# Three edits to one core's conformer block: where the first up-projection sums stand on VectorE, where a third pair of up products runs, and where one down-projection weight is split

## The chip, the cores and the metric

The kernel runs on one core of one Trainium2 chip. The metric is the device time of one execution in microseconds; it is given as a median over runs. Every time of a single instruction comes from one execution that the hardware profiler recorded. The engines are called as the profile calls them: PE (TensorE matmul), PEld (TensorE weight load), DVE (VectorE), ACT (ScalarE), POOL (GpSimd), SP (SyncE, which here only starts DMA transfers; its queue is shown as SPq).

## The reference

One conformer block on x of 1 x 1024 tokens x 1024 channels, float32 throughout, one layer:

```python
h = rms_norm(x, norm1_g)
glu_in, q, k, v, gate_logits = split(h @ w_in)
a = a_val * sigmoid(a_gate)
a = silu(rms_norm(causal_depthwise_conv(a, conv_w, conv_b), conv_norm_g))   # 31 taps
y_a = a @ w_conv_out
y_b = o @ w_attn_out          # o: 16 heads, three dilation groups mixed by softmax of their lse
g_a, g_b = split(sigmoid(gate_logits + gate_b))
x = x + (g_a * y_a + g_b * y_b) @ w_out
h = rms_norm(x, norm2_g)
u = causal_depthwise_conv(h @ w_up, ffn_conv_w, ffn_conv_b)                 # 3 taps, 5632 columns
u_val, u_gate = split(u)
x = x + (silu(u_gate) * u_val) @ w_down                                     # 2816 rows
```

The edits lie in the last third: the merge of the two branches and `w_out`, the up projection, and the start of the down projection.

## The kernel before, in words

**Products of float32.** Each operand is split into a high part and a low part (`split`, L74 to L77: ACT copies the high part to the fp32r type at L76, DVE subtracts it from the source at L77), and each product is three matmuls: high by high, high by low, low by high. Weights come from memory in pieces of 128 x 1024 (`stage`, L81), and pass through three tags of four buffers each: `raw`, `whi`, `wlo`. PSUM has two tiles of two banks (`big_ps`) and four single banks (`bank_ps`).

**Engines and order.** All DMA transfers are started by SP, one queue in program order. Every engine works through its own program in order. Most of that order is made by a planner when the kernel is built, from the written order, the costs it assumes and the free buffers; so an instruction may stand ahead of one that was written before it. Two things bind it: inside `tc.manual_schedule` (L797 to L891) ACT, DVE and PE keep the written order, and `tc.issue_after(ins)` puts what is written under it behind `ins`. Where a buffer is used again, the new writer waits for the last reader.

**Merge and w_out.** `merge(c, w, half)` (L607 to L625) loads two gates and y_a for eight channel blocks and two halves of the tokens (L611 to L613), takes two sigmoids (L614, L615), multiplies y_a by its gate (L616), computes y_b with PE, multiplies it by the other gate (L623), adds (L624) and splits the sum into `mT`, the left operand of `w_out`. `wo_piece(j, i)` (L627 to L637) stages a quarter of half of `w_out` and splits it (L632 ACT, L633 DVE). The merges of the last two blocks are followed by the token loop `for tt in range(8)` (L718 to L722): 24 matmuls (L125 to L127) for each of eight token tiles and the first 512 columns, added to x (L704), written to `dx2`. A second round, over the second 512 columns, ends with the norm and scaling (`wo_scaled`, L715) and the transposes (`transpose_raw`, L686, copied out at L687).

**Forms ahead.** The up projection takes each pair of column tiles (f and 22 + f, 256 columns in all) by seven products of a 512 x 128 weight block with a 512 x 512 activation block in place of eight, which needs sums of weight blocks. For f = 0 and 1 these sums are made ahead, during `w_out`: `forms_ahead(f)` (L653 to L678) loads two pieces, forms sums on DVE (L661), splits them and spills the parts to memory (`dform`), from which `fetched` brings them back later. For f = 1 the plain piece is split and spilled too.

**Up projection.** A tile has two plain products (`up_first`, L752: 12 matmuls each into two banks, X and Z) and five with sums (`y` and `xz` at L740 to L742). The right operands are sums of the activations, held in blocks t1, t2, t3, t4, b22 (high part on ACT at L791, low part on DVE at L794, the sums at L822). The hand-ordered stretch makes these blocks for the first half of the tokens, transposes the last two token tiles (x6, x7), runs the plain products of f = 1 (`xz1`), makes the second half of the blocks, and then runs the five products of f = 0 (`y_0`, then the X products; `xc`, L877, copies a product out of its bank before the next one adds to it). From then on tiles run one behind another: `up_rest` (L910 to L931; its last copy out of a bank is L930), with `up_weights`, `up_first` and `up_sums` (L760 to L771) for the tile after it.

**Start of the down projection.** Before the last up tile two pairs of `early` tiles load and split the first two groups of activations. Then, for each group of two feature tiles, `wload` (L933 to L941) loads a piece of `w_down`, `wsplit` splits it through `whi` and `wlo` (`hi_a`, `lo_a`), and `mac` (L993, tiles `dx` and `dy`) multiplies; the third group's activations are split into `gh` and `gl`.

## Time and profile before

| | |
|---|---|
| median of 3 runs | 1802.28 us (1801.72 to 1803.02) |
| profiled execution | 1801.54 us |
| its span | 1799.8 us |
| mean granted TensorE clock | 0.996 |
| PE | 1764.8 us busy, 98%, 8248 instructions |
| DVE | 1314.3 us busy, 73%, 1805 |
| ACT | 770.4 us busy, 43%, 1203 |
| POOL | 182.9 us busy, 10%, 193 |
| DMA | 270.16 MB, mean 150 GB/s |

The span runs from the first to the last instruction that the profiler recorded; the execution's time has 1.7 us around it. A row of the timeline reads: start and length in us, engine, line and operation, result <- operands by the program's names, shapes, how many such instructions stand together, and in brackets how long the engine had been idle before it and what released it. A row of the windows view gives a stretch, its length, then the busy time (and count) of PE, PEld, DVE, ACT and POOL, the granted clock of PE (1.00 is full), the share of time that the DMA engines worked, and GB/s. A matmul's own length overlaps with the next one's; the distance between starts is what it costs.

### The profile page before, as it was taken

The numbers are of one execution on the slowest core, as the hardware profiler recorded it, in microseconds if no ns is written. First come the engines' busy times: TensorE is split into PE (matmuls) and PEld (weight loads), VectorE is DVE, ScalarE is ACT, GpSimd is POOL, SyncE is SP. The second block draws the span as 40 slices with busy tenths as digits, with TensorE's granted clock in tenths as the row PEclk, the third lists the DMA queues.
The fourth block names the chain that finished last, engine by engine and source line by source line (L and its number), as shares of the span: only waits on it lengthen the run. The fifth ranks groups of instructions, "written<-read, shape, count | busy, mean of one in ns | idle before, by whom it ended". The sixth has DMA issues, their size and how long they took to land.

```text
span 1799.8 us, 22541 instructions
## 1 busy us (share of the span) xinstructions
PE 1764.8 (98%) x8248; PEld 1460.0 (81%) x8248; DVE 1314.3 (73%) x1805; ACT 770.4 (43%) x1203; POOL 182.9 (10%) x193
## 2 busy tenths in 40 slices
PE   8999999999999999999999989999999999999999
PEld 6888888888887888878888878778888888878887
DVE  6999999999635666665654554687777677679863
ACT  5111132232246666665654333455454454543431
POOL 1000132133003222122210000000000000000000
PEclk9999999999999999999999999999999999999999
DMA  5111145345468546674527556532222222389851
GB/s 205 50 52 51 39 137 171 104 138 161 146 207 250 141 137 182 197 210 135 153 71 268 180 205 242 193 105 91 85 71 94 83 78 86 118 322 330 289 181 47
DMA packets 145809, 270.16 MB, mean 150 GB/s; under 512 B 11681, under 2 KB 60961, under 8 KB 145698
## 3 DMA queue, kind: packets, MB, share of 16 engines
q1 hardware_dynamic: 145696, 268.72, 46.1%
q8 instruction: 65, 1.06, 0.2%
q14 instruction: 46, 0.38, 0.1%
q10 hardware_dynamic: 2, 0.00, 0.0%
HBM read 196.32 MB, written 72.35 MB: 149 GB/s over the span
## 4 chain that ended last, share of the span: by engine, by line
PE 55%; DVE 4%; DMA 3%; ACT 1%; issue 1%; SPq 0%; POOLq 0%; DVEq 0%; ACTq 0%
PE dx L993 6%; PE xz L741 5%; PE xz L740 5%; PE xz L742 5%; PE dy L993 5%; DMA gg<-dya 2%; PE pp L524 2%; PE y L741 2%; PE y L740 2%; PE y L742 2%; PE ya L108 2%; PE ya L109 2%; PE ya L110 2%; PE o L532 2%; PE o L533 1%; PE wo L126 1%
## 5 line engine op out<-in xcount | busy, mean ns | idle before, releaser
L367 DVE SCALAR_TENSOR_TENSOR cacc<-apad,pk,cacc 128x1024 f32<-128x1024 f32 x240 | 297.9, 1276 | 0.7
L125 PE MATMUL qkv<-hi_qkv,hT 128*128 128x512 f32 x384 | 151.9, 397 | 0.0
L127 PE MATMUL qkv<-hi_qkv,hT 128*128 128x512 f32 x384 | 150.5, 392 | 0.0
L126 PE MATMUL qkv<-lo_qkv,hT 128*128 128x512 f32 x384 | 149.5, 390 | 0.0
L513 DVE CUSTOM_DVE_ANT_0 p<-s,m 128x128 f32<-128x128 f32 (+7 forms) x128 | 95.1, 750 | 62.5 <-PE pp L524 42.7
L77 DVE TENSOR_TENSOR pl<-pp,ph 128x512 fp32r<-128x512 f32 x192 | 102.9, 550 | 47.6 <-ACT ph L76 47.0
L76 ACT ACTIVATE ph<-pp 128x512 fp32r<-128x512 f32 x192 | 91.2, 488 | 94.7 <-PE pp L524 92.0
L517 POOL TENSOR_SCALAR p<-p,st 128x128 f32<-128x128 f32 (+7 forms) x128 | 95.2, 753 | 332.5 <-DVE st L516 269.8
L903 DVE SCALAR_TENSOR_TENSOR u<-u,pk 128x1023 f32<-128x1023 f32 x88 | 112.2, 1276 | 2.7 <-ACT u L901 2.5
L101 POOL TENSOR_TENSOR rs<-ss,mhalf 128x8 f32<-128x8 f32 x32 | 73.8, 2312 | 337.9 <-DVE ss L100 337.9
L515 ACT ACTIVATE p<-p,st 128x128 f32<-128x128 f32 (+7 forms) x128 | 99.0, 776 | 14.9 <-DVE st L513 13.1
L108 PE MATMUL gate<-hT,hi_gt 128*128 128x512 f32 x256 | 101.5, 396 | 0.0
L109 PE MATMUL gate<-hT,hi_gt 128*128 128x512 f32 x256 | 100.5, 393 | 0.0
L110 PE MATMUL gate<-hT,lo_gt 128*128 128x512 f32 x256 | 100.0, 392 | 0.0
L524 PE MATMUL pp<-ident,p 128*128 128x128 f32 x576 | 93.8, 276 | 0.0
L127 PEld LDWEIGHTS qkv<-hi_qkv,hT 128*128 128x128 f32 x384 | 72.1, 188 | 15.4
L126 PEld LDWEIGHTS qkv<-lo_qkv,hT 128*128 128x128 f32 x384 | 72.2, 188 | 14.4
L125 PEld LDWEIGHTS qkv<-hi_qkv,hT 128*128 128x128 f32 x384 | 72.2, 188 | 14.0
L77 DVE TENSOR_TENSOR lo_uv<-raw_uv,hi_uv 128x1024 fp32r<-128x1024 f32 x21 | 25.7, 1226 | 78.2 <-ACT hi_uv L76 78.2
L524 PEld LDWEIGHTS pp<-ident,p 128*128 128x128 f32 x576 | 69.1, 141 | 10.0 <-issue 0.2
L532 PE MATMUL o<-ph,v 128*128 128x512 f32 x192 | 73.0, 380 | 3.9 <-ACT ph L76 1.7
L508 PE MATMUL s<-kh,q 128*128 128x512 f32 (+1 forms) x192 | 68.4, 361 | 7.3 <-DVE st L513 7.2
(307 smaller groups left out, 4632.8 us busy)
## 6 DMA issues: line engine op xcount, KB each, us to landing
wr<-w_down SPq DMA_DIRECT2D x45, 512.0 KB, 5.5
gr<-dff SPq DMA_DIRECT2D x62, 256.0 KB, 5.1
raw_qkv<-w_qkv SPq DMA_DIRECT2D x24, 512.0 KB, 3.9
dff<-u SPq DMA_DIRECT2D x22, 512.0 KB, 2.6
raw_uv<-w_up SPq DMA_DIRECT2D x21, 512.0 KB, 3.2
raw_ug<-w_up SPq DMA_DIRECT2D x20, 512.0 KB, 3.2
dv<-v SPq DMA_DIRECT2D x16, 512.0 KB, 3.2
raw_gt<-w_ch SPq DMA_DIRECT2D x16, 512.0 KB, 4.6
```

What stands on the lines that cost most here:

```text
L77: dve.tensor_tensor(out=lo, in0=src, in1=hi.bitcast(F32), op=ALU.subtract)
L108: pe.matmul(o, hi[:, k, :], ah[:, k, :], start=(k == 0), stop=False)
L109: pe.matmul(o, hi[:, k, :], al[:, k, :], start=False, stop=False)
L110: pe.matmul(o, lo[:, k, :], ah[:, k, :], start=False, stop=(k == KT - 1))
L125: pe.matmul(ps, ah, hi[:, k % 2, :], start=(k == 0), stop=False)
L126: pe.matmul(ps, ah, lo[:, k % 2, :], start=False, stop=False)
L127: pe.matmul(ps, al, hi[:, k % 2, :], start=False, stop=(k == KT - 1))
L367: dve.scalar_tensor_tensor(out=acc, in0=a[:, j : j + T], scalar=w(j), in1=acc, op0=ALU.mult, op1=ALU.add)
L524: pe.transpose(pp[:, qb * P : (qb + 1) * P], pts[qb][:, kt * P : (kt + 1) * P], ident)
L740: pe.matmul(o, wh[:, k, :], bh[:, k, :], start=(start and k == 0), stop=False, skip_group_check=not start)
L741: pe.matmul(o, wh[:, k, :], bl[:, k, :], start=False, stop=False, skip_group_check=not start)
L993: pe.matmul(banks[n], a[:, c], b[:, d], start=(start and i == 0 and m == 0), stop=(stop and i == nf - 1 and m == 2), skip_group_check=True)
```

## The change

Three edits.

1. `merge` returns the two instructions of its split. `forms_ahead` is called after token tiles 0, 2 and 3 (for f = 0, 1, 2) and everything it issues on an engine is queued behind the two split instructions of the last merge (block 7, second half).
2. `forms_ahead(2)` only loads the plain piece of f = 2, splits it and spills its two parts. The hand-ordered stretch fetches them (`w2`) and runs that pair's 24 matmuls into two single banks (`xz2`) between `xz1` and `y_0`. The transposes of x6 and x7 are written between the halves of `xz1`, ahead of the high part of t2; the low part of t2's first half is written later, behind the second half's first low part. For f = 2 the loop then only makes the sums, without its own `up_weights` and `up_first`.
3. The two `early` tiles get a fourth row. Before the last up tile the second group's first weight piece is loaded and split into those rows; its place among the `whi` and `wlo` buffers at the start of the down projection goes.

By engine, the program has as many PE and DVE instructions as before, and five more DMA transfers on SP: one load, two spills and two fetches.

```diff
@@ gate and memory tiles
-    dform = [[dr.tile([P, 1024], F32R, name=f"dform{f}_{i}") for i in range(7)] for f in range(2)]
+    dform = [[dr.tile([P, 1024], F32R, name=f"dform{f}_{i}") for i in range(7)] for f in range(3)]
@@ merge
-                split(mT[0][half][:, c, :], mT[1][half][:, c, :], ya)
+                hi, lo = mT[0][half][:, c, :], mT[1][half][:, c, :]
+                return (act.activation(hi, ya, AF.Copy),
+                        dve.tensor_tensor(out=lo, in0=ya, in1=hi.bitcast(F32), op=ALU.subtract))
...
-            merge(7, ws[3], 1, lambda b: wo_first.append(wo_piece(0, 3, b)))
+            merged = merge(7, ws[3], 1, lambda b: wo_first.append(wo_piece(0, 3, b)))
@@ forms_ahead
-            v, g = stage(w_up[f], f"fv{f}"), stage(w_up[FT + f], f"fg{f}")
-            t = hb2.tile([P, 4, 1024], F32R, tag=f"hb{f}1", name=f"form{f}")
-            r = hb2.tile([P, 4, 1024], F32R, tag="hb10", name=f"formr{f}")
+            v = stage(w_up[f], f"fv{f}")
+            r = hb2.tile([P, 4, 1024], F32R, tag="hb00" if f == 2 else "hb10", name=f"formr{f}")
+            if f < 2:
+                g = stage(w_up[FT + f], f"fg{f}")
+                t = hb2.tile([P, 4, 1024], F32R, tag=f"hb{f}1", name=f"form{f}")
+            else:
+                g = v
...
             if f:
                 split(r[:, 2], r[:, 3], v)
+            if f == 2:
+                for i in range(2):
+                    spill(dform[f][5 + i], r[:, 2 + i])
+                return
...
-            if tt in (0, 2):
-                forms_ahead(tt // 2)
+            if tt in (0, 2, 3):
+                with tc.issue_after(merged[0].ins), tc.issue_after(merged[1].ins):
+                    forms_ahead((tt + 1) // 2)
@@ up projection
+        def up_half(o, w, i):
+            product(o, four(w[0])[:, 4 * i : 4 * i + 4], four(w[1])[:, 4 * i : 4 * i + 4], *left[i], True)
...
             w1 = fetched(1, 5, "uv")
+            w2 = fetched(2, 5, "uv")
...
+            transpose_raw(x6, 6)
+            xz1 = big_ps("xz_1")
+            up_half(xz1[:, 0:512], w1, 0)
+            transpose_raw(x7, 7)
+            up_half(xz1[:, 512:1024], w1, 1)
             high("t2", t3[0], q)
             act.activation(xc[:, 0:512], xz0[:, 0:512], AF.Copy)
-            transpose_raw(x6, 6)
-            transpose_raw(x7, 7)
-            low("t2", t3[0], q)
...
-            xz1 = up_first(1, w1)
+            xz2 = [bank_ps(f"xz_2{i}") for i in range(2)]
+            for i in range(2):
+                up_half(xz2[i], w2, i)
...
             low("t1", t1[1], q)
+            low("t2", t3[0], cols[0])
             high("b22", b22[:, :, cols[0]], cols[0])
...
-            X, Z = xz[:, 0:512], xz[:, 512:1024]
+            X, Z = xz if f == 2 else (xz[:, 0:512], xz[:, 512:1024])
@@ loop over the up tiles
-        early = []
+        early, rooms = [], []
...
-                    e = hb2.tile([P, 3, 1024], F32R, tag=f"hb{a}1", name=f"early{a}")
+                    e = hb2.tile([P, 4, 1024], F32R, tag=f"hb{a}1", name=f"early{a}")
+                    rooms.append(e[:, 3])
...
+                split(*rooms, wload(0, 0, groups[1], wp))
...
-                if 1 < f + 1 < FT:
+                if f == 1:
+                    ready.append((xz2,) + up_sums(2, stage(w_up[2], "uv2")))
+                elif 2 < f + 1 < FT:
                     v, w = up_weights(f + 1)
                     ready.append((up_first(f + 1, w),) + up_sums(f + 1, v))
@@ down projection, first loop
-            w = wload(0, 0, fs, wp)
-            if fs is groups[1]:
+            if fs is not groups[1]:
+                w = wload(0, 0, fs, wp)
+            else:
                 rs11 = [residual(0, n, 0) for n in range(4)]
             g = early.pop(0) if early else gsplit(gload(0, 0, fs), f"b11_{fs[0]}")
-            first2.append((g, wsplit(w, f"a11_{fs[0]}")))
+            first2.append((g, rooms if fs is groups[1] else wsplit(w, f"a11_{fs[0]}")))
```

More of the change, by code (lines that the diff above doesn't have):

```diff
@@ L750, in up_weights @@
             return v, wsplit(v, f"uv{f}")
+        def up_half(o, w, i):
+            product(o, four(w[0])[:, 4 * i : 4 * i + 4], four(w[1])[:, 4 * i : 4 * i + 4], *left[i], True)
         def up_first(f, w):
-            vh, vl = w
             xz = big_ps(f"xz_{f}")
-            product(xz[:, 0:512], four(vh)[:, 0:4], four(vl)[:, 0:4], *left[0], True)
-            product(xz[:, 512:1024], four(vh)[:, 4:8], four(vl)[:, 4:8], *left[1], True)
+            for i in range(2):
+                up_half(xz[:, i * 512 : i * 512 + 512], w, i)
             return xz
@@ L851, in block_kernel @@
             blk = {n: (t[:, 0], t[:, 1]) for n, t in blocks.items()}
-            xz1 = up_first(1, w1)
+            xz2 = [bank_ps(f"xz_2{i}") for i in range(2)]
+            for i in range(2):
+                up_half(xz2[i], w2, i)
             q = cols[1]
```

## The prediction

> **What bounds the kernel now.** I read the page's first lines, then the table of what TensorE (PE) waited for over the whole run, then PE's, DVE's and ACT's timelines around each wait that the diff can touch.

> ```profile
> PE 1764.8 (98%) x8248; PEld 1460.0 (81%) x8248; DVE 1314.3 (73%) x1805; ACT 770.4 (43%) x1203; POOL 182.9 (10%) x193
> ```

> PE is busy 98% of the span, and by the built program the change leaves its instructions as many as they were. So time can come only from places where PE stands or its clock is low. In the waits (total us, times, longest) three places belong to the edited lines:

> ```profile
> PE wo L126 <- DVE lo_wo L633: 4.6, 1, 4.6
> PE tq L686 <- issue: 1.7, 1, 1.7
> PE dx L993 <- ACT u L930: 1.4, 1, 1.4
> PE y L741 <- DVE blk_t L794: 0.8, 1, 0.8
> PE xz L741 <- DVE blk_t L794: 0.8, 1, 0.8
> PE xz L740 <- ACT blk_t L791: 0.7, 1, 0.7
> PE xz L740 <- ACT xc L877: 0.7, 1, 0.7
> PE dx L993 <- DVE gl_b L77: 0.4, 1, 0.4
> PE dx L993 <- ACT gh_b L76: 0.3, 1, 0.3
> ```

> They are A, the start of w_out (4.6); C, the hand-ordered start of the up projection (`tq`, `y`, `xz`, 4.7 named); D, the start of the last projection (`dx`, 2.1). Every profile time below is on the clock of the profiled execution, 1801.54 us, 0.74 under the runs' median of 1802.28.

> **A. Form sums tied behind merge 7.** DVE runs in its programmed order; so does PE.

> ```profile
> 1055.08 0.68 DVE L623 TENSOR_TENSOR gg<-yb,gg 128x512 f32<-128x512 f32 x1
> 1060.20 0.69 DVE L661 TENSOR_TENSOR formr<-raw_fg 128x512 f32<-128x512 f32 x1 [4.44 <-DMA raw_fg<-w_up]
> 1060.81 0.68 DVE L624 TENSOR_TENSOR gg<-gg 128x512 f32<-128x512 f32 x1
> 1061.41 1.22 DVE L633 TENSOR_TENSOR lo_wo<-raw_wo,hi_wo 128x1024 fp32r<-128x1024 f32 x1
> ...
> 1057.67 0.39 PE L125 MATMUL wo<-hi_wo,mT 128*128 128x512 f32 x1
> 1062.68 0.79 PE L126 MATMUL wo<-lo_wo,mT 128*128 128x512 f32 x1 [4.62 <-DVE lo_wo L633]
> ...
> 1068.67 0.39 PE L127 MATMUL wo<-hi_wo,mT 128*128 128x512 f32 x1
> ...
> 1757.89 5.44 PE dy L993 x24
> ```

> A form sum (L661) waited 4.44 for its w_up piece and held up the merge and lo_wo_2, for which PE then stood 4.62. Afterwards PE ran at half pace. From the row of 24 in the chain of waits, an undisturbed matmul costs 5.44 / 24 = 0.2267. The one at 1068.67 is the 15th after the one at 1057.67, so undisturbed it begins at 1057.67 + 15 x 0.2267 = 1061.07: 7.60 are lost here, 4.6 standing and 3.0 slow. The windows view shows the slow part as granted clock (0.57, behind POOL's pair):

> ```profile
> 1062.60:1069.40 6.80, 6.72 (x18) 5.29 (x19) 6.80 (x10) 3.25 (x4) 0.00 (x0) 0.57 0.72 211
> ```

> With L661 behind both splits of merge 7, L624 follows L623 at 1055.7 and lo_wo_2 is done at 1057.55; PE wants it at 1057.90. What is late next is piece 3, behind merge 7 on ACT:

> ```profile
> 1054.95 0.39 PE L125 MATMUL wo<-hi_wo,mT 128*128 128x512 f32 x1
> ...
> 1052.97 0.42 SPq L613 DMA_DIRECT2D gg<-dya  x1
> ...
> gg<-dya SPq DMA_DIRECT2D x1, 256.0 KB, 5.9
> ...
> 1058.28 0.63 ACT L615 ACTIVATE gg<-gg 128x512 f32<-128x512 f32 x1 [1.51 <-DMA gg<-dgate]
> 1062.06 1.04 ACT L632 ACTIVATE hi_wo<-raw_wo 128x1024 fp32r<-128x1024 f32 x1
> ```

> Merge 7's own transfers do not move: its second sigmoid still starts at 1058.28, dya still lands at 1052.97 + 5.9 = 1058.9. After the sigmoid ACT has a 0.5 copy and then hi_wo_3, about 1059.35 to 1060.4; PE's first matmul with it is the 24th, due at 1054.95 + 23 x 0.2267 = 1060.16. That leaves 0.3. lo_wo_3 ends at 1061.7, due at 1061.8. A stand of 0.3 instead of 4.62 should leave the clock alone. Gain 7.6 - 0.3 = **7.3**, bounds 4.5 (the slow clock comes anyway) and 7.6.

> [...]

> What this costs elsewhere: the form operations start about 4 us later, and behind their spills on the single SP queue stand the raw pieces of w_out's second round.

> ```profile
> 1090.71 0.73 SPq L81 DMA_DIRECT2D raw_wo<-w_o  x1
> ...
> raw_wo<-w_o SPq DMA_DIRECT2D x4, 512.0 KB, 8.0
> ...
> DMA packets 7347, 18.92 MB, mean 236 GB/s; under 512 B 816, under 2 KB 816, under 8 KB 7344
> ...
> GB/s 0 223 264 216 334 11 25 242 294 181 332 418 422 416 405 299 349 312 411 393 324 334 406 385 129 181 179 69 306 98 202 343 39 228 165 131 0 262 131 0
> ...
> 1106.10 0.84 PE L125 MATMUL wo<-hi_wo,mT 128*128 128x512 f32 x3
> ```

> The last of them now lands at 1090.71 + 8.0 = 1098.7. In the built order about 2.1 MB more stands ahead of it (part C's load and two spills, and some x2 traffic). The 2-us slices from 1060 to 1064 moved 11 and 25 GB/s; filled at 0.37 MB/us, the mean of the slices from 1084 to 1098, they take 1.5 MB. So it lands 0.6 / 0.37 = 1.6 us later, at 1100.3, or 5.7 later, at 1104.4, if nothing is made up. The round itself moves from 1106.10 to 1098.8, and wants the last lo_wo with its 31st matmul, at 1105.6. Before that come 1.04 (L632) and 1.22 (L633): landing is in time up to 1103.3. Price 0 to 1.1; I take 0, since the near end has 3 us in hand.

> **C. A third plain pair in the hand-ordered stretch.**

> ```profile
> 1122.59 0.87 PE tq L686 x8
> ...
> 1161.07 1.03 PE L686 MATMUL tq<-ident,x 128*128 128x128 f32 x8
> 1163.83 1.06 PE L686 MATMUL tq<-ident,x 128*128 128x128 f32 x8 [1.73 <-issue]
> ...
> 1180.17 0.40 PE L741 MATMUL xz<-blk_t,hi_s3g 128*128 128x512 f32 x1
> ```

> From 1161.07 to 1180.17 PE takes 19.10. Its work there is two sets of 8 transposes, 0.87 each by the chain's row, and 24 + 12 + 12 + 1 = 49 matmuls: 1.74 + 11.11 = 12.85. So 6.25 are lost, to five waits and the restarts behind them. The change moves 24 matmuls of tile 2 (5.44) from later into this stretch, ahead of `y_0`, and puts half of xz1 between the two sets of transposes. x7 was there for its transposes at 1163.83, and twelve matmuls put them at 1161.07 + 0.87 + 2.72 = 1164.66; what DVE and ACT owe to `y_0` and the first X product is due 5.4 later. So four of the waits close; the wait for xc (L877), behind PE's own product, stays with about 1.0 and its restart. After: 12.85 + 5.44 + 1.0 = 19.3. The stretch takes 0.2 more and 5.44 of work are gone from tile 2: gain **5.2**, bounds 0 and 6.25 (xc closes too).

> What hides it: ACT and DVE must keep up.

> ```profile
> 1166.40 2.05 ACT L687 ACTIVATE h2raw<-tq 128x512 f32<-128x512 f32 x4
> 1170.35 2.36 DVE L794 TENSOR_TENSOR blk_t<-cb_t,blk_t 128x1024 fp32r<-128x1024 f32 x2
> ...
> 1154.83 0.42 SPq L133 DMA_DIRECT2D lo_uv<-dform  x1
> ...
> lo_uv<-dform SPq DMA_DIRECT2D x1, 512.0 KB, 6.2
> ```

> The second transposes now end at about 1165.5, ACT's copies (0.51 each) at 1166.5. Then come eight DVE operations of 1.18 (two took 2.36), the last being the second low of t2: ready at 1166.5 + 8 x 1.18 = 1175.9. PE wants it after 61 matmuls, at 1161.07 + 1.74 + 61 x 0.2267 = 1176.64. The margin is 0.7; beyond it each microsecond costs one. xz1's low part lands at 1154.83 + 6.2 = 1161.0, due at about 1162.4; the third pair's follows by about 1162.3, due at 1168.3. In the tiles behind (f = 1 to 3) PE is 5.4 ahead of where it was:

> ```profile
> 1200.00:1300.00 100.00, 100.00 (x442) 82.53 (x441) 77.52 (x88) 47.65 (x57) 0.00 (x0) 1.00 0.24 84
> ```

> DVE (third pair: 77.5% busy, ACT 47.7%) has room there; walking the built order to 1221 left at least 0.4 at every meeting.

> **D. Last projection.** The second group's weight split leaves the start of the stage for idle ACT and DVE time about 25 us earlier.

> ```profile
> 1588.61 1.06 ACT L76 ACTIVATE hi_a<-wr 128x1024 fp32r<-128x1024 f32 x1 [6.60 <-PE xz L741]
> 1590.21 0.50 PE L993 MATMUL dx<-hi_a,early 128*128 128x512 f32 x1 [1.41 <-ACT u L930]
> ```

> The largest wait is for L930, which empties a bank and stands on ACT behind a hi_a copy, which itself waits for a weight slot that PE frees at 1588.6. The change removes one such copy, but in the built order the next one takes its place ahead of L930. So 1.41 stays. Of the two small waits (0.33, 0.44) some 0.3 go, because a half-size copy now stands ahead of the third group's split. Gain **0.3**, bounds 0 and 2.2.

> **Sum.** 7.3 + 5.2 + 0.3 = 12.8; 1801.54 - 12.8 = 1788.7, and 0.74 more for the median: about 1789.5. With the upper bounds of all three, 16.05, it is 1786.2.

> **Rivals.**
> - DVE and ACT become the bound of the first up tiles: low t2 or L930's chain comes late by what PE runs ahead, and C's 5.2 go. For it: the margins of 0.4 and 0.7. Against: DVE's share of 77%. 1789.5 + 5.2 = 1794.7.
> - A wait takes the place of A's: hi_wo_3 or merge 7's dya comes late enough for the slow clock to follow, which keeps 2.8. For it: 1060.4 against 1060.16, with transfers not mine to fix. Against: it is 0.3 beside 4.62. 1792.3.
> - Slower: the spills starve the second w_out round. From the first spill, about 1066.7, 19 pieces of 0.524 MB and seven of 0.262 stand in the queue up to its last raw piece: 11.8 MB. At the window's mean of 236 GB/s instead of 0.37 MB/us that is 50 us: 1116.7, and with L632 and L633 1119, 13.4 after 1105.6; a slow clock of 2.8 follows. 16.2 - 12.8 = 3.4 slower, 1805.7. It decides from a landing past 1113.3 on, where 10.0 + 2.8 eat the gain. Against it: the same queue held 300 to 420 GB/s from 1070 to 1098.
> - The change does nothing: each wait meets the next late thing and the time stays at 1802.3. Against: in A and C what is late next is counted above.

> **How the numbers follow.** Forecast 0.61, DVE-bound tiles 0.13, a kept slow clock 0.13, starved w_out 0.08, nothing 0.05. A measurement can tell about 0.2% (3.6 us) from no change: faster means below 1798.7, which the first three share, 0.87. Nothing and the lighter part of starving make 0.08, its heavier part 0.05. The likeliest case alone spans 1786.5 to 1792; the range reaches up to 1797, where the two dearer faster cases fall together (5.2 + 2.8 = 8.0 more, 1797.5).

> **What would show it.** A: no wait at L126 above 0.5 near 1058, granted clock 1.00 in the following 7 us, w_out's second round near 1098.8 without a new wait. C: `y_0` starting about 7.3 + 0.2 earlier than before though 24 matmuls were put ahead of it, only xc left of the five waits; between 1180 and 1221 no wait of PE on L794 or L930 above 0.4. D: the 1.4 for L930 still there. Wrong would be a PE wait for lo_wo around 1100, for blk_t around 1170, or a low granted clock behind either.

## The result, and the profile after

| | before | changed |
|---|---|---|
| median, first comparison | 1802.0 us (4 runs, 1801.66 to 1803.02) | 1789.24 us (4 runs, 1786.84 to 1790.98) |
| ratio, first comparison | | 0.9927, 95% interval 0.991 to 0.9945 |
| median, second comparison | 1798.77 us (29 runs, 1794.89 to 1806.12) | 1789.96 us (6 runs, 1789.48 to 1791.12) |
| ratio, second comparison | | 0.9945, 95% interval 0.9926 to 0.9963 |
| profiled execution (its span) | 1801.54 us (1799.8) | 1790.98 us (1789.2) |

The kernel is faster, by less than 1%: both intervals stay below 1, and both hold 0.9926 to 0.9945, which is 10 to 13 us. By their medians the first comparison gives 12.8 us and the second 8.8; the second's ratio on record, 0.9945, is 9.9 us. Two views of the changed kernel's profile stand first: the busy line, and what PE waited for, from the first w_out matmul to the end.

```profile
PE 1761.9 (98%) x8248; PEld 1459.5 (82%) x8248; DVE 1314.4 (73%) x1805; ACT 770.9 (43%) x1203; POOL 183.8 (10%) x193
```

```profile
PE dx L1016 <- ACT u L949: 1.4, 1, 1.4
...
PE xz L751 <- ACT xc L896: 0.7, 1, 0.7
...
PE tq L696 <- ACT wo L716: 0.3, 1, 0.3
PE dx L1016 <- ACT gh_b L76: 0.3, 1, 0.3
PE dx L1016 <- DVE gl_b L77: 0.2, 1, 0.2
```

The 4.6 us at L126 are gone, four of the five waits in C are gone, and in D the 1.4 stays while two small ones shrink from 0.77 to about 0.5. Since every instruction of PE is still there, this should be visible as distances between the same matmuls. They are taken from PE's timeline: the first w_out matmul, the first transpose of x6, the second matmul on the first s3g weights, the first dx matmul on gl_b. Here are the changed kernel's rows.

```profile
1058.06 0.39 PE L125 MATMUL wo<-hi_wo,mT 128*128 128x512 f32 x1
...
1156.57 1.03 PE L696 MATMUL tq<-ident,x 128*128 128x128 f32 x8
...
1160.21 1.04 PE L696 MATMUL tq<-ident,x 128*128 128x128 f32 x8
...
1175.58 0.50 PE L751 MATMUL xz<-blk_t,hi_s3g 128*128 128x512 f32 x1 [0.69 <-ACT xc L896]
1175.92 0.40 PE L752 MATMUL xz<-blk_t,hi_s3g 128*128 128x512 f32 x1
...
1580.23 0.50 PE L1016 MATMUL dx<-hi_a,early 128*128 128x512 f32 x1 [1.41 <-ACT u L949]
...
1587.70 0.50 PE L1016 MATMUL dx<-hi_a,gl_b 128*128 128x512 f32 x1 [0.25 <-DVE gl_b L77]
```

| part of the span | before | changed | difference |
|---|---|---|---|
| to the first w_out matmul | 1054.95 | 1058.06 | +3.11 |
| A: to x6's transposes | 106.12 | 98.51 | -7.61 |
| C: to the second matmul on s3g (24 matmuls more) | 19.10 | 19.35 | +0.25 |
| tiles, to the first dx matmul on gl_b (24 fewer) | 417.74 | 411.78 | -5.96 |
| to the end | 201.89 | 201.50 | -0.39 |

The sum is -10.60, the difference of the spans (1789.2 - 1799.8). Behind the first w_out matmul the two executions differ by 13.7; the changed one gave 3.1 back ahead of all edits, in a stretch that no edit touches. By an estimate from the time at half clock, the clock explains 1.7 of these 3.1 (the section on the hardware); the rest stays open. The 7.6 of part A is more than other executions of the kernel before lose there, as the experiments show.

In A the windows view of the changed kernel has PE busy throughout and the clock at 1.00, where before it stood 4.6 us and then ran at 0.57:

```profile
1055.00:1062.00 7.00, 7.00 (x33) 5.79 (x32) 5.95 (x9) 4.32 (x6) 0.00 (x0) 1.00 0.96 308
1062.00:1069.00 7.00, 7.00 (x33) 5.79 (x32) 6.23 (x10) 2.65 (x4) 0.00 (x0) 1.00 0.60 198
```

The third rival's place, the SP queue ahead of w_out's second round, held. The last raw piece was issued at 1092.18 and no such piece took longer than 8.6 to land:

```profile
1092.18 1.12 SPq L81 DMA_DIRECT2D raw_wo<-w_o  x1
...
DMA to landing us min/median/max: 6.6/7.2/8.6
```

So it was there by 1100.8, 42.7 us behind the first w_out matmul. The prediction allowed 1103.3 - 1054.95 = 48.35.

### The profile page after: what moved, and what is told of

The parts are those of the page before. It is cut to its first block, busy times and chain, and to the rows that moved or that the text cites. A ratio compares the mean times of both kernels' runs of the same rounds, so it can differ in the third digit from the quotient of the medians.

```text
span 1789.2 us, 22563 instructions
## 1 busy us (share of the span) xinstructions
PE 1761.9 (98%) x8248; PEld 1459.5 (82%) x8248; DVE 1314.4 (73%) x1805; ACT 770.9 (43%) x1203; POOL 183.8 (10%) x193
## 3 DMA queue, kind: packets, MB, share of 16 engines
q8 instruction: 65, 1.06, 0.3%
## 5 line engine op out<-in xcount | busy, mean ns | idle before, releaser
L125 PE MATMUL qkv<-hi_qkv,hT 128*128 128x512 f32 x384 | 151.9, 397 | 0.0
L127 PE MATMUL qkv<-hi_qkv,hT 128*128 128x512 f32 x384 | 150.5, 392 | 0.0
L126 PE MATMUL qkv<-lo_qkv,hT 128*128 128x512 f32 x384 | 149.5, 390 | 0.0
L77 DVE TENSOR_TENSOR pl<-pp,ph 128x512 fp32r<-128x512 f32 x192 | 102.9, 550 | 48.7 <-ACT ph L76 48.0
L76 ACT ACTIVATE ph<-pp 128x512 fp32r<-128x512 f32 x192 | 91.0, 487 | 96.1 <-PE pp L524 93.5
L127 PEld LDWEIGHTS qkv<-hi_qkv,hT 128*128 128x128 f32 x384 | 72.1, 188 | 15.4
L126 PEld LDWEIGHTS qkv<-lo_qkv,hT 128*128 128x128 f32 x384 | 72.2, 188 | 14.4
L125 PEld LDWEIGHTS qkv<-hi_qkv,hT 128*128 128x128 f32 x384 | 72.1, 188 | 14.1
L77 DVE TENSOR_TENSOR lo_uv<-raw_uv,hi_uv 128x1024 fp32r<-128x1024 f32 x20 | 24.5, 1226 | 79.9 <-ACT hi_uv L76 79.9
## 6 DMA issues: line engine op xcount, KB each, us to landing
wr<-w_down SPq DMA_DIRECT2D x45, 512.0 KB, 5.9
gr<-dff SPq DMA_DIRECT2D x62, 256.0 KB, 5.5
raw_qkv<-w_qkv SPq DMA_DIRECT2D x24, 512.0 KB, 4.1
dff<-u SPq DMA_DIRECT2D x22, 512.0 KB, 2.6
raw_uv<-w_up SPq DMA_DIRECT2D x21, 512.0 KB, 3.3
raw_ug<-w_up SPq DMA_DIRECT2D x20, 512.0 KB, 3.2
dv<-v SPq DMA_DIRECT2D x16, 512.0 KB, 3.2
raw_gt<-w_ch SPq DMA_DIRECT2D x16, 512.0 KB, 4.8
```

What stands on the lines that cost most here:

```text
L77: dve.tensor_tensor(out=lo, in0=src, in1=hi.bitcast(F32), op=ALU.subtract)
L125: pe.matmul(ps, ah, hi[:, k % 2, :], start=(k == 0), stop=False)
L126: pe.matmul(ps, ah, lo[:, k % 2, :], start=False, stop=False)
L127: pe.matmul(ps, al, hi[:, k % 2, :], start=False, stop=(k == KT - 1))
```

## The experiments

Runs of one kernel differ by several us, so each kernel's own profile is read by the distances above; each kernel is described below the table. The table has them in us, from the start times of the same matmuls; a median of few runs tells less. "Ratio" is to runs of the kernel before on the same chip, with its interval.

| kernel | first w_out matmul | A | C | to gl_b | median | ratio |
|---|---|---|---|---|---|---|
| e1_sums_alone | 1056.51 | 99.65 | 19.10 | 417.70 | 1794.7 (12) | 0.9973 (0.9961 to 0.9984) |
| e2_pair_alone | 1058.67 | 103.20 | 19.35 | 412.03 | 1792.37 (12) | 0.9967 (0.9955 to 0.998) |
| e3_rooms_alone | 1055.74 | 103.67 | 19.12 | 417.48 | 1799.87 (12) | 1.0004 (0.9992 to 1.0017) |
| e4_after_again | 1056.85 | 98.49 | 19.29 | 411.54 | 1789.96 (6) | 0.9945 (0.9926 to 0.9963) |
| e5_interleave_alone | 1052.98 | 103.88 | 18.76 | 418.13 | 1800.02 (10) | 1.0008 (0.9997 to 1.0018) |
| e6_pair_not_interleaved | 1056.16 | 98.48 | 21.20 | 411.80 | 1790.96 (10) | 0.9954 (0.9942 to 0.9966) |
| e9_two_more_lows | 1054.54 | 98.46 | 21.27 | 411.89 | 1790.76 (5) | 0.996 (0.9946 to 0.9974) |
| e10_spare_spills | 1056.74 | 105.22 | 19.35 | 411.41 | 1794.77 (10) | 0.9976 (0.9963 to 0.9989) |
| e7_stand_of_2 | 1060.33 | 98.99 | 19.28 | 411.71 | 1793.65 (6) | 0.9965 (0.9953 to 0.9976) |
| e8_stand_of_4 | 1056.11 | 99.50 | 19.35 | 411.70 | 1789.81 (4) | 0.9944 (0.993 to 0.9957) |
| e11_evict_first | 1058.72 | 98.53 | 19.35 | 411.85 | 1788.59 (4) | 0.9936 (0.9921 to 0.9951) |
| e14_banks_and_fill | 1060.62 | 98.50 | 19.28 | 416.35 | 1800.38 (11) | 1.0004 (0.9994 to 1.0014) |

### The three parts, one at a time, and the whole again

**Part A alone** puts the tie on the kernel before and nothing else:

```diff
             if tt in (0, 2):
-                forms_ahead(tt // 2)
+                with tc.issue_after(merged[0].ins), tc.issue_after(merged[1].ins):
+                    forms_ahead(tt // 2)
```

> The kernel before with part A alone. By the prediction PE's 4.6 us at L126 goes and with it the half clock: from the first w_out matmul to the transposes of x6 it takes 98.5 to 98.8 us in place of 106.1, and the median falls by 7.3 to 7.6, to about 1794.5. The rival, by which the slow clock has another cause (the transfers of that time, the change from one product to the next), keeps the slow 2.8 to 3.0 us and gives 4.6 less, about 1797.4. C's waits stay as they were (4.7 us named), D's too.

A took 99.65. A wait of 0.9 for lo_wo was left, and the clock stayed at 1.00 around and behind it:

```profile
1060.51 0.50 PE L126 MATMUL wo<-lo_wo,mT 128*128 128x512 f32 x1 [0.89 <-DVE lo_wo L635]
```

```profile
1054.00:1061.00 7.00, 6.11 (x27) 4.76 (x26) 6.93 (x10) 3.62 (x6) 0.00 (x0) 1.00 0.72 257
1061.00:1068.00 7.00, 7.00 (x33) 5.77 (x32) 6.23 (x10) 2.19 (x4) 0.00 (x0) 1.00 0.84 260
```

So the mechanism is the predicted one and the rival, which kept the slow clock, is out. It is the trace that says so: 0.9973 is 4.9 us (2.9 to 7.0), and the medians differ by 4.1, which is nearer to the rival's 4.6 than to 7.3. Two things make the gain smaller. The 0.89 that is left comes, as far as the trace shows, from a transfer again: ACT waited 3.90 for a gate of the merges until 1050.34, and DVE then worked without a gap from 1052.50 to the end of that low part at 1060.45. And the profile that the 7.3 was read from was a dear one, as the next kernels show.

**Part C alone** is the changed kernel without the tie and without the rooms for the second group's split:

```diff
-                with tc.issue_after(merged[0].ins), tc.issue_after(merged[1].ins):
-                    forms_ahead((tt + 1) // 2)
+                forms_ahead((tt + 1) // 2)
...
-                split(*rooms, wload(0, 0, groups[1], wp))
```

> The kernel before with part C alone (third form, third plain pair, transposes between the halves of xz1). By the prediction the stretch from the transposes of x6 to the second matmul on s3g takes 19.3 to 19.4 us with 24 matmuls more, tile 2 is 5.4 shorter and the median falls by 5.2, to about 1796.8; the 4.6 at L126 stays, with its slow clock. The rival by which DVE and ACT bind in the first tiles leaves waits of PE on L794 and L930 of together 5 us between 1180 and 1230 and a median at 1802.

C took 19.35, its forecast; from 1180 to 1260 the only wait of PE was the 0.7 for xc; the ratio is 5.9 us (3.6 to 8.1). DVE and ACT did not bind. But A, which is here as in the kernel before, took 103.20 and not 106.12. Here are its wait, and the windows on both sides of the time at which its clock fell:

```profile
1064.56 0.50 PE L126 MATMUL wo<-lo_wo,mT 128*128 128x512 f32 x1 [2.79 <-DVE lo_wo L635]
```

```profile
1062.39:1065.80 3.41, 1.24 (x5) 1.05 (x6) 3.41 (x6) 2.17 (x3) 0.00 (x0) 1.00 0.11 23
1065.80:1069.21 3.41, 3.41 (x9) 2.64 (x8) 3.41 (x6) 2.16 (x3) 0.00 (x0) 0.50 0.69 237
1069.21:1072.62 3.41, 3.41 (x16) 2.79 (x15) 3.41 (x5) 0.46 (x1) 0.00 (x0) 1.00 0.99 214
```

PE stood 2.79, not 4.62, and the clock was at half for 3.41 us, from 1065.80 to 1069.21, where the kernel before has twice that (its rows are in the section on the hardware). The same stand was 3.3 in e3_rooms_alone and 3.5 in e5_interleave_alone. From 1050 to 1150 the clock was 0.98 in these three, and 0.97 in the kernel before:

```profile
1062.14 0.78 PE L126 MATMUL wo<-lo_wo,mT 128*128 128x512 f32 x1 [3.29 <-DVE lo_wo L633]
...
1059.55 0.50 PE L126 MATMUL wo<-lo_wo,mT 128*128 128x512 f32 x1 [3.46 <-DVE lo_wo L633]
```

Four executions without the tie thus lost, against the changed kernel's 98.5: 7.6, 4.7, 5.2 and 5.4. The one that the prediction was made from is the dearest of them.

**Part D alone** is the third edit of the change put on the kernel before (the diff's hunks on `early`, `rooms` and `first2`).

> The kernel before with part D alone. By the prediction the wait of 1.4 us for L930 stays, gh_b and gl_b wait 0.3 less together, and the median falls by 0.2 to 0.3, which the runs cannot tell from nothing. The rival by which the weight slot causes L930's delay takes that wait away too: 1.7 to 2.2 less.

From the second matmul on s3g to gl_b it took 417.48 instead of 417.74, and the waits of the first projection became the changed kernel's:

```profile
PE dx L995 <- ACT u L930: 1.4, 1, 1.4
PE dx L995 <- ACT gh_b L76: 0.3, 1, 0.3
PE dx L995 <- DVE gl_b L77: 0.2, 1, 0.2
```

That is 0.26, and the runs tell no difference (1.0004). The rival by which the freed weight slot takes the 1.4 away is out.

**The changed kernel again**, unedited.

> The changed kernel as it is, five more runs. Its four runs so far lie near 1787.2 and near 1790.9. If that is the clock in the attention stretch, ahead of every edit, the profile's granted clock between 640 and 660 us and between 800 and 820 us goes with the span: one slow stretch less is about 1.7 to 2 us less, and the distances behind the first w_out matmul stay within 0.1 us of the profile at hand (98.5 to the transposes of x6, 19.35 to the second matmul on s3g). If it is the edits, these distances differ by 3 us.

A and C took 98.49 and 19.29, within 0.06 of the first profile; the way to gl_b 0.24 less. So the edits' distances repeat in these two executions. But its six runs lie between 1789.5 and 1791.1 and show no second cluster, and the first w_out matmul stood at 1056.85 with the clock at 0.91 in both windows of the attention stretch: the two clusters of the first four runs were not seen again.

### Where C's gain comes from

**The order alone**, on the kernel before: x6's transposes, half of xz1, x7's transposes, the other half, then the high part of t2; its low part behind the second half's first low part.

```diff
+            transpose_raw(x6, 6)
+            xz1 = big_ps("xz_1")
+            up_half(xz1[:, 0:512], w1, 0)
+            transpose_raw(x7, 7)
+            up_half(xz1[:, 512:1024], w1, 1)
             high("t2", t3[0], q)
...
-            transpose_raw(x6, 6)
-            transpose_raw(x7, 7)
-            low("t2", t3[0], q)
...
-            xz1 = up_first(1, w1)
```

> The kernel before with only the order of C: x6's transposes, half of xz1, x7's transposes, the other half, no third pair. If what PE waits for in this stretch is the chain from x7's transposes over ACT's copies and DVE's blocks, as the prediction has it, the wait of 1.7 at L686 goes and the waits at y_0 and the X products grow by as much: the stretch takes 19.1 to 19.9 us, nothing gained, up to 0.8 lost since x7 is transposed 0.8 later. If the 1.7 was a loss of its own the stretch takes about 17.2 and the median falls by 1.9.

The wait at L686 went, and the others grew:

```profile
PE xz L740 <- ACT blk_t L794: 1.8, 1, 1.8
PE xz L741 <- DVE blk_t L797: 0.8, 1, 0.8
PE y L741 <- DVE blk_t L797: 0.8, 1, 0.8
PE xz L740 <- ACT xc L882: 0.7, 1, 0.7
PE y L740 <- ACT blk_t L794: 0.4, 1, 0.4
```

Together 4.5 where they were 4.7; C took 18.76, 0.3 under the kernel before and just below the range expected, but the tiles behind it took 0.39 longer (418.13 against 417.74); the runs tell no difference. The 1.7 was no loss of its own.

**The third pair without that order**: the changed kernel with the two sets of transposes side by side again.

> The changed kernel with x6's and x7's transposes side by side again, ahead of all of xz1, third pair kept. By the prediction's account the 1.7 at L686 and its restart come back and nothing else does: the stretch takes 21.1 to 21.4 us in place of 19.35, the median is 1.7 to 2.0 above the changed kernel's. If DVE's chain set y_0's start anyway, nothing changes.

C took 21.20, 1.85 more than the changed kernel, and the added wait is the one named:

```profile
PE tq L696 <- issue: 1.7, 1, 1.7
PE xz L751 <- ACT xc L894: 0.7, 1, 0.7
```

So the order gains 1.9, but only together with the pair that makes everything behind it due later.

**The margin of DVE**: the low part of t1's second half computed three times.

```diff
-            low("t1", t1[1], q)
+            for _ in range(3):
+                low("t1", t1[1], q)
```

> The changed kernel with the second half's low part of t1 computed three times in place of once (the same values): DVE has 2.3 us more to do ahead of the second low part of t2. By the prediction the margin there is 0.7, so PE waits about 1.6 at the first X product and restarts in 0.3: 1.6 to 2.0 us more, all at that place, and nothing later since DVE stood 2.3 us just behind. If DVE were no cover (another engine sets the start), nothing; if DVE bound already, 2.3 or more.

C took 21.27, 1.92 more. In the changed kernel the second low part of t2 ran from 1170.24 for 1.23, so it was there at 1171.47; PE took it at 1172.24, the second matmul of that X product. The margin was 0.77 for a forecast of 0.7. With 2.36 more work PE waits 0.77 for it, and 0.60 for the high part ahead of it:

```profile
1169.20 0.49 PE L751 MATMUL xz<-blk_t,hi_s 128*128 128x512 f32 x1 [0.60 <-ACT blk_t L804]
1170.46 0.50 PE L752 MATMUL xz<-blk_t,hi_s 128*128 128x512 f32 x1 [0.77 <-DVE blk_t L807]
```

Beside these 1.37 the two waits cost another 0.55 in restarts (1.92 - 1.37): behind the second the next matmul started only 0.34 later, at 1170.80, where matmuls otherwise stand 0.23 apart. The way to gl_b took 411.89: nothing was late behind it.

### The queue ahead of w_out's second round

```diff
             for i in range(4):
                 spill(dform[f][i], t[:, i])
+                spill(dspare[f][i], t[:, i])
```

> The changed kernel with eight spills more (4.2 MB, the four form parts of f = 0 and 1 written a second time to memory that nobody reads) ahead of w_out's second round on the SP queue. At 0.37 MB per us the last raw piece lands about 11 us later; it landed about 5 us ahead of its need. So by the prediction's third rival PE waits 5 to 7 us for hi_wo or lo_wo at the second round's first tile and its clock falls behind it: 8 to 10 us more. If the queue has room to run faster, the piece lands within 5 us of its old time and nothing changes.

A took 105.22, 6.7 more, with two waits of 1.8 and the slow clock behind them:

```profile
PE wo L125 <- ACT hi_wo L636: 1.8, 1, 1.8
PE wo L125 <- ACT wo L719: 1.8, 1, 1.8
```

```profile
1100.00:1104.00 4.00, 2.19 (x10) 1.50 (x9) 0.69 (x1) 0.72 (x2) 0.00 (x0) 1.00 1.04 414
1104.00:1108.00 4.00, 2.17 (x7) 1.22 (x6) 0.22 (x1) 1.13 (x2) 0.00 (x0) 0.53 1.02 409
1108.00:1112.00 4.00, 3.96 (x11) 2.67 (x12) 3.99 (x4) 2.04 (x2) 0.00 (x0) 0.62 0.62 242
```

The second stand is the rival's: for hi_wo, whose raw piece ACT had waited 3.15 for. The first is for a bank that ACT frees (L719) behind DVE, which had waited 3.33 for a block of x from the same queue; the prediction did not name that way. With the slow clock both prices of the rival are there (3.6 of named stands; the other 3.1 in restarts and the slow clock, 0.53 and 0.62 from 1104 to 1112). But these are 4.2 MB more than the change has, and even they leave the kernel faster than the one before. The size was expected 1.3 to 3.3 too high: PE stood 3.6, not 5 to 7. The DMA engines were busy throughout from 1100 to 1108 (a share of 1.02 to 1.04, 409 to 414 GB/s), so the queue had no room there.

### The stand by itself: two experiments that missed

To see from which stand on the clock falls, the third piece's low part was computed four times (and six times) in place of once, in `wo_piece`:

```diff
+            for _ in range(1 + extra):
-            low_ = dve.tensor_tensor(out=lo, in0=raw, in1=hi.bitcast(F32), op=ALU.subtract)
+                low_ = dve.tensor_tensor(out=lo, in0=raw, in1=hi.bitcast(F32), op=ALU.subtract)
```

> The changed kernel with the third w_out piece's low part computed four times in place of once (the same values), so that DVE hands it over 3.4 us later; it had 1.7 in hand, so PE stands about 1.7 at L126. If the clock falls with a stretch of low activity of some length, as the runs with stands of 2.8 to 4.6 suggest (each lost 1.9 to 3.0 beyond the stand), 1.7 is near the edge: the clock stays at 1.00 and the stretch from the first w_out matmul to the transposes of x6 takes 100.2 to 100.6. If every stand that is seen in a window of the clock's own costs it, 102 to 102.5, with a slow part that begins up to a few us behind the stand.

> The same with six times in place of once: DVE is 5.7 later and PE stands about 4.0, without a form sum or a transfer being late. By the prediction's reading (the stand alone makes the clock fall) the slow part follows as in the kernel before, 2 to 3 us, and the stretch takes 104.5 to 105.5. If the slow clock belonged to the transfers or the form sums around the stand, 102.5.

PE did not stand at L126 in the first and stood 0.69 in the second, at 1065.80, 9.7 us behind w_out's first matmul; the clock stayed at 1.00. The planner knows what DVE has to do: by the built programs the first product with that piece's low part is w_out's 14th in the kernels before and after, and the 29th and 40th in these two. A takes 0.5 and 1.0 more. So neither says anything on stands of 2 to 4 us. They do show that work written into DVE's order need not end up as a wait of PE, since the planner can put other products ahead; the form sum's 4.4 for a transfer did end up there.

### Trying for more

**The copy out of the bank first.**

```diff
+            with ExitStack() as behind:
+                if fs is groups[4]:
+                    behind.enter_context(tc.issue_after(last.ins))
```

(`last` is the copy at L949; the weight split of that group follows inside.)

> The changed kernel with ACT's copy of the fifth group's weights (hi_a_8) behind the last copy out of the last up tile's bank (L930, here L949). By the prediction's reading of D the wait of 1.4 falls to the 0.7 of an unobstructed copy (as at xc); but what ACT does next (the silu's chain, then gh_b) is no earlier, so the wait for gh_b grows from 0.3 to about 1.0 and the distance from the second matmul on s3g to the first on gl_b stays at 411.6 to 411.9. If the copy's place is all that counts, 0.7 to 1.4 less.

```profile
PE dx L1017 <- ACT gh_b L76: 1.1, 1, 1.1
...
PE dx L1017 <- ACT u L949: 0.7, 1, 0.7
PE dx L1017 <- DVE gl_b L77: 0.3, 1, 0.3
```

1.4 + 0.3 became 0.7 + 1.1, and the way to gl_b took 411.85: the wait only moved, as expected. The median of 1788.59 is not told apart from the changed kernel's, since the two intervals overlap.

**Other banks, and three matmuls as a fill.**

```diff
-        X = [t[:, h * 512 : h * 512 + 512] for t in xs_ for h in range(2)]
-        Y = [bank_ps(f"dy_{n}") for n in range(4)]
+        X = halves(big_ps("dx_0")) + [bank_ps(f"dx_{n}") for n in range(2, 4)]
+        Y = halves(big_ps("dy_0")) + [bank_ps(f"dy_{n}") for n in range(2, 4)]
```

The last three matmuls of the third pair were also written between the X products on t2 and t3, and the fifth and sixth groups' weight splits behind the third group's gh_b and gl_b.

> The changed kernel with two edits more. First, the last three matmuls of the third pair run between the X products on t2 and t3, in xc's wait: the stretch from x6's transposes to the second matmul on s3g takes 18.4 to 18.8 in place of 19.3. Second, the first projection's banks are drawn so that two of them are single banks that no late copy holds, and the fifth and sixth group's weight splits stand behind the third group's gh_b and gl_b: the wait of 1.4 goes and gh_b is early enough, so that from the second matmul on s3g to the first on gl_b it takes 409.8 to 410.5 in place of 411.7. Together 1.8 to 2.6 less than the changed kernel, 1787.4 to 1788.2 beside 1790.0. If gh_b or its transfer is what sets D, only the first 0.7 comes.

Both parts failed; the kernel is as slow as the one before (1.0004).

```profile
PE dx L1024 <- ACT gh_b L76: 5.1, 1, 5.1
PE dx L1024 <- ACT gh_t L76: 2.5, 1, 2.5
PE xz L751 <- ACT xc L900: 0.6, 1, 0.6
```

```profile
1176.93 0.60 ACT L943 ACTIVATE u<-xz 128x512 f32<-128x512 f32 x1 [1.29 <-DVE blk_b L807]
1177.42 0.59 ACT L900 ACTIVATE xc<-xz 128x512 f32<-128x512 f32 x1
...
1585.37 0.60 ACT L955 ACTIVATE u<-xz 128x512 f32<-128x512 f32 x1 [10.61 <-PE xz L753]
```

The fill: the next tile's copy (L943) now stands ahead of xc's on ACT, and xc's wait is back at 0.6; C takes 19.28. The banks: freed of the late copy, the planner put most of the early products ahead of the last up product, from 1576.33 on. Behind that product only 1.8 us of them were left while ACT and DVE worked from it to gh_b, and PE waited 5.1. The 5.4 us of early products behind the 1.4 wait had been gh_b's cover. Around the 5.1 the clock was 0.58 from 1590 to 1595 and 0.74 from 1595 to 1600, which makes 6.8 us at half; behind the 2.5, which ended at 1617.81, matmuls stood 0.43 apart, where at a clock of 1.00 they stand 0.23. None of the kernels tried beats the changed one.

## Why the prediction was right

1789.5 was forecast for the median; 1789.24 and 1789.96 were measured. The mechanisms held, but that the number fits so closely is partly luck: the three runs of before that it starts from (median 1802.28) lie 3.5 above the second comparison's 29 (1798.77), and its 12.8 is 2.9 more than that comparison's ratio gives and 4.0 more than its medians. The two errors cancel. By its own steps:

- **A, 7.3.** The step stood: lo_wo_2 no longer waits, no wait above 0.5 near 1058, the clock at 1.00, and in the two profiles compared it is 7.6, since the 0.3 left for hi_wo_3 did not appear. That merge 7's transfers do not move was not so: its second sigmoid, put at 1058.28, started at 1059.48 and in e4_after_again at 1057.36, and hi_wo_3 was there 3.5 and 2.6 us behind w_out's first matmul, not 5.45. As a number for the median 7.3 was too large. The 4.62 standing and 3.0 slow were read off one execution of the kernel before; three others lost 4.7, 5.2 and 5.4, so the mean of four is 5.7, and part A alone gained 4.9 by its ratio, with 1.1 of its own left in its profile. The slow part was as uncertain as the stand: beyond it the three others lost 1.9 each, where the prediction had 3.0. The rows of L661 say where the stand's spread comes from: DVE waited 4.4 to 4.8 for raw_fg in all four, but the sum starts 5.25, 3.41, 3.91 and 4.08 behind w_out's first matmul, and PE's stand is 0.6 less than that each time. Whether PE or the transfer was early or late was not separated.
- **C, 5.2.** 19.35 against 19.3 forecast, in this and e2_pair_alone; 5.44 - 0.25 = 5.2. That the four waits close because all is due 5.4 later, and that x7's transposes need the twelve matmuls ahead of them, are shown by e5 and e6; the margin of DVE by e9.
- **D, 0.3.** 0.26 in e3_rooms_alone; the 1.4 stayed, as said. e14 shows what it covers, which the prediction didn't see.
- **The queue.** Forecast to be in time, and it was, by 5.6 us (48.35 - 42.7), where 3 were counted on. e10 shows the rival is a real one.
- **Not forecast:** 0.6 us more between C and the end, in gaps too small for the list of waits (5.96 - 5.44 - 0.26 = 0.26, and 0.39 behind gl_b), and the 3.1 that the profiled execution lost ahead of w_out.

## What to carry to other kernels

A wait read from one execution is one draw: where its end is set by a transfer, compare the same stretch in several profiles before it becomes a term of a sum. Where no such wait lies between them, distances between the same matmuls repeated within 0.06 us (A and C of the changed kernel) to 0.24 us (the way to gl_b), while runs of the kernel before scatter by 11; so an edit of 1 us can be judged by them. A wait that PE pays may be the cover of the next one: before removing it, ask what PE would do in that time and what it would then meet.

## What the runs showed of the hardware

```profile
1058.25:1061.66 3.41, 0.00 (x0) 0.00 (x0) 1.46 (x3) 0.76 (x2) 0.00 (x0) 1.00 0.44 175
1061.66:1065.07 3.41, 2.39 (x6) 1.90 (x7) 3.41 (x6) 3.10 (x4) 0.00 (x0) 0.50 0.36 124
1065.07:1068.49 3.42, 3.42 (x10) 2.65 (x9) 3.42 (x5) 1.08 (x2) 0.00 (x0) 0.50 0.79 256
```

The clock fell at 1061.66, while PE still stood; in e2_pair_alone it fell at 1065.80, 1.24 us behind the restart. What both have ahead of the fall is a window in which PE worked little: 0.00 and 1.24 of 3.41. The traces of the kernel before and of the changed one have about 1030 such windows from 14 us on. In five of those at full clock PE worked 0.00 to 1.49 us, two of them at the end, and all five were followed by 0.50. In three it worked between 1.69 and 1.81: those from 645.24 (1.80) and 1160.65 (1.69) of the kernel before were followed by 1.00, the one from 802.25 (1.81) by 0.50. In all others it worked 1.96 or more, and none was followed by 0.50. The 0.89 of e1_sums_alone leaves PE at work in 2.52 of any 3.41 us around it, and the clock stayed at 1.00 from 1054 to 1068. That it counts where a stand falls in these windows, beside how long it is, would fit; no run moved a stand and left its length. Two executions show the same place ahead of every edit with two outcomes, the changed kernel's first and e5_interleave_alone:

```profile
645.46:648.87 3.41, 1.49 (x11) 1.10 (x9) 3.41 (x6) 2.27 (x5) 0.18 (x1) 1.00 0.77 186
648.87:652.28 3.41, 3.36 (x13) 3.12 (x14) 2.82 (x11) 2.70 (x7) 1.83 (x2) 0.50 1.04 273
```

```profile
644.52:647.93 3.41, 1.83 (x13) 1.40 (x11) 3.41 (x4) 2.25 (x5) 0.55 (x1) 1.00 0.65 168
647.93:651.34 3.41, 2.99 (x18) 2.64 (x19) 3.35 (x13) 3.33 (x9) 1.47 (x2) 1.00 1.05 272
```

PE worked 1.49 in one window and 1.83 in the other, and only the first was followed by half clock. Ahead of w_out the changed kernel's first execution has 10.24 us at half clock; in e5_interleave_alone the clock is 1.00 in every 100 us from 400 to 1000. An estimate from this, half of the 10.24, is 5.1 us lost, the size of 1058.06 - 1052.98 = 5.1, the difference of their first w_out matmuls. The kernel before has 6.83 there, so 1.7 of the 3.1 between before and changed is clock. It is not the only cause: with half of the time at half clock taken off (3.4 us each), the first w_out matmul would still lie at 1051.1 in e9_two_more_lows and at 1055.3 in e2_pair_alone. Most of the scatter of whole runs goes with the clock. Of the 71 runs of the kernel before in the later comparisons, the four with a mean clock of 1.000 took 1794.85 to 1795.05 us, and the five with 0.995, which is about 9 us lost, 1803.30 to 1806.12. By the same estimate 3.41 us at half clock are 0.001 of the mean, so in those four there was no such stretch, not at A either. Four runs of part A alone are at 1.000 too and took 1792.11 to 1792.96: without a fall of the clock on either side, A is worth 2 to 3 us.
